# Sums of a visit taken out of PSUM by ScalarE and added by GpSimd, and the shift and scale accumulated in PSUM

## The chip, the cores and the metric

The kernel runs on one core of a Trainium2 chip. The metric is the device time of one execution in microseconds (us). Three executions of the kernel before took 1558.4, 1559.89 and 1560.08 us; the median is 1559.89 us. Engines are named as in the profile: PE is TensorE, PEld its weight load, DVE is VectorE, ACT is ScalarE, POOL is GpSimd, SP is SyncE, whose queue issues the transfers.

## The reference, cut to what matters

One decoder layer on 256 rows of 4096 numbers, all in float32:

```
mod = silu(c) @ w_ada + b_ada                       # 4096 x 12288, one row
shift, scale, gate = split(mod, 3)
h = rmsnorm(x, norm_gain) * (1 + scale) + shift     # 256 x 4096
proj = h @ w_in                                     # 4096 x 12288: q k v g_attn u_pool g_pool
y_attn = longnet_mixture(q, k, v) * silu(g_attn)    # 16 heads, 3 dilation patterns
y_pool = multiscale_pool(u_pool, w_pool, pool_scale) * silu(g_pool)
x = x + gate * (concat(y_attn, y_pool) @ w_out)     # 4096 x 4096
out = rmsnorm(x, final_gain)
```

`h` needs the first two thirds of `silu(c) @ w_ada`, and nothing of `h @ w_in` can start on a slice of `h` before shift and scale of that slice are known.

## The kernel before, in words

The 4096 columns of `h` are cut into 16 **units** of 256. For each unit the kernel needs 256 columns of shift and 256 of scale. They come from `w_ada` in 16 tasks (`ada_tasks`): a task loads two transfers of 256 KB into a `raw` tile, and later (`ada_acc`, L161) VectorE does two multiply-adds of 128x512, `aacc = raw * cact + aacc`. The 128 partial sums of each column lie on the 128 partitions. `build_h` (L203) then adds them over the partitions: four products with a column of ones on TensorE (L208, recorded as eight instructions), three small VectorE operations (L211 to L213) that make shift and scale, two ScalarE activations that make the slice of `h` in float32 (L221), and its split into a high part `hh` (ScalarE, L223) and a low part `hl` (VectorE, L224).

`h @ w_in` has 24 output chunks of 512 columns. A **piece** is 256 rows of one chunk of weights, 512 KB: one transfer into a `raw` tile, a cast to the high part `wh` (ScalarE, L237), the low part `wl = raw - wh` (VectorE, L238), and 12 products of 128x512 on TensorE (L248): eight with `wh`, then four with `wl`. There are three `wh`, three `wl` and seven `raw` buffers; the `raw` ring is shared with the tasks of `w_ada`.

The 24 chunks are **visited** in turn, round after round. A visit (L276) takes the pieces of all units that are ready and that this chunk has not had yet, and sums them in a PSUM tile `mm` of 128x1024 (two buffers). The first visit of a chunk ends with a ScalarE copy of the sums into SBUF (L289); each later one ends with a VectorE add to the sums kept there (L291: `accs = mm + accs`). This phase, "phase one" below, has 327 pieces. A last round of 24 visits, in which attention and pooling are interleaved, and the output product follow.

How fast the tasks of `w_ada` are asked for is set by a table: `ada_hook` is called once per piece, adds `2 * RATES[units built]` to a credit, and issues tasks while the credit is positive; a task costs `0.728 * 2 = 1.456`. When the last task of a unit has been issued, `build_h` is called, and two pieces later the unit is ready (`LAG`). With the table of before, `build_h` is called for units 1, 2, 3, 4, ... 15 after 14, 29, 52, 77, ... 325 pieces, and that is also where the products L208 stand among TensorE's instructions.

The order on each engine is made by a scheduler with its own cost model when the program is built. An engine then works through its own instructions strictly in that order, and an instruction that has to wait holds up all that stand behind it on its engine.

```
RATES = (0.8, 0.8, 0.8, 0.5, 0.46, 0.5, 0.5, 0.5, 0.48, 0.5, 0.5, 0.54)
ADA_COST = 0.728 * PIECE
```

Of the kernel before, what the change touches and what calls it, by code (L numbers as in the profile page):

```python
# [7 lines left out]
F32 = mybir.dt.float32  # L8
F32R = mybir.dt.float32r
AF = mybir.ActivationFunctionType  # L10
ALU = mybir.AluOpType
AX = mybir.AxisListType

P = 128
S = 256
NT = S // P
D = 4096
KT = D // P
CH = 512
# [8 lines left out]
NU = len(UNITS)  # L28
US = [sum(UNITS[:i]) for i in range(NU + 1)]
HB = 2  # L30
A0 = 1
WIN = 5
LAG = 2
RATES = (0.8, 0.8, 0.8, 0.5, 0.46, 0.5, 0.5, 0.5, 0.48, 0.5, 0.5, 0.54)
DEPTH = 3
HOLD = 1
EARLY = 4
# [18 lines left out]
def tile_hybrid_block(  # L56
# [17 lines left out]
    nc = tc.nc  # L74
    PSUM = bass.MemoryType.PSUM

    const = ctx.enter_context(tc.tile_pool(name="const", bufs=1))
# [12 lines left out]
    def misc():  # L90
        return ps_m.tile([P, CH], F32, name="psm")

    def raw_tile():
        return strm.tile([P, RAW], F32, name="raw", bufs=RAWB)
# [7 lines left out]
    ident = const.tile([P, P], F32, name="ident")  # L102
# [1 line left out]
    colB = const.tile([P, 2 * KT], F32, name="colB")  # L104
    ones_r = const.tile([P, P], F32R, name="ones_r")
    cact = const.tile([P, KT], F32, name="cact")
    ones = const.tile([P, 1], F32, name="ones")
    gb = const.tile([P, KT], F32, name="gb")
    ssq = const.tile([P, NT, 8], F32, name="ssq")
    rr = const.tile([P, NT], F32, name="rr")  # L110
# [5 lines left out]
    adap = ada_cm.enter_context(tc.tile_pool(name="ada", bufs=2, side="right"))  # L116
# [6 lines left out]
    NR = 3 * KT + 16  # L123
    nc.sync.dma_start(out=rows[0:KT], in_=c.rearrange("b (k p) -> (b k) p", p=P))
    nc.sync.dma_start(out=ident, in_=k_ident)
    nc.vector.memset(ones, 1.0)
    pt = misc()
    nc.tensor.transpose(out=pt[:, 0:KT], in_=rows[0:KT], identity=ident[0:KT, 0:KT])
    nc.scalar.activation(out=cact, in_=pt[:, 0:KT], func=AF.Silu)
# [25 lines left out]
    def ada_acc(acc, rt, kts, width, init=None):  # L155
        for i, kt in enumerate(kts):
            r = rt[:, i * width:(i + 1) * width]
            if kt == 0 and init is None:
                nc.vector.tensor_scalar(out=acc, in0=r, scalar1=cact[:, 0:1], scalar2=None, op0=ALU.mult)
            else:  # L160
                nc.vector.scalar_tensor_tensor(out=acc, in0=r, scalar=cact[:, kt:kt + 1],  # L161
                                               in1=init if kt == 0 else acc,
                                               op0=ALU.mult, op1=ALU.add)
# [3 lines left out]
    def late_work(f, lag=None):  # L167
        delayed.append(f)
        while len(delayed) > (HOLD if lag is None else lag):
            delayed.pop(0)()  # L170

    def flush_work():
        while delayed:
            delayed.pop(0)()

    def ada_tasks(u, pool):
        w = 2 * UNITS[u] * P
        n = RAW // w
        cs = slice(US[u] * P, US[u + 1] * P)
        acc = []  # L180
        tasks = []
        for a in range(0, KT, n):
            kts = list(range(a, min(KT, a + n)))

            def f(kts=kts):
                if not acc:
                    acc.append(pool.tile([P, 2 * HB * P], F32, name="aacc")[:, 0:w])
                rt = raw_tile()
                m = len(kts)
                v = rt[:, 0:m * w].rearrange("p (n s d) -> p n s d", n=m, s=2)  # L190
                if m == 1:
                    nc.sync.dma_start(out=v[:, 0], in_=wa_v[:, kts[0], 0:2, cs])
                else:
                    for i in range(2):
                        nc.sync.dma_start(out=v[:, :, i], in_=wa_v[:, kts[0]:kts[-1] + 1, i, cs])
                late_work(lambda: ada_acc(acc[0], rt, kts, w))
            tasks.append(f)
        return acc, tasks
# [4 lines left out]
    def build_h(u, acc, pool, xT):  # L203
        flush_work()
        uk, k0 = UNITS[u], US[u]
        pc = misc()
        for j in range(2 * uk):
            nc.tensor.matmul(pc[:, j:j + 1], lhsT=acc[:, j * P:(j + 1) * P], rhs=ones, start=True, stop=True)  # L208
        s12 = const.tile([P, 2, HB], F32, name="s12", bufs=2)
        ks = slice(k0, k0 + uk)  # L210
        nc.vector.tensor_tensor(out=s12[:, 0, 0:uk], in0=pc[:, 0:uk], in1=colB[:, ks], op=ALU.add)  # L211
        nc.vector.tensor_tensor(out=s12[:, 1, 0:uk], in0=pc[:, uk:2 * uk], in1=gainc[:, ks], op=ALU.mult)
        nc.vector.tensor_tensor(out=s12[:, 1, 0:uk], in0=s12[:, 1, 0:uk], in1=gb[:, ks], op=ALU.add)  # L213
        for a in range(0, uk, 2):
            kk = k0 + a
            if kk % HB == 0:
                htile[kk // HB] = [pool.tile([P, HB, S], F32R, name=n, align_bytes=LINE) for n in ("hh", "hl")]
            hh, hl = [v[:, kk % HB:kk % HB + 2] for v in htile[kk // HB]]
            hf = strm.tile([P, 2, S], F32, name="hf")
            for i in range(2):  # L220
                nc.scalar.activation(out=hf[:, i], in_=xT[:, kk + i], func=AF.Identity,  # L221
                                     scale=s12[:, 1, a + i:a + i + 1], bias=s12[:, 0, a + i:a + i + 1])
            nc.scalar.copy(out=hh, in_=hf)  # L223
            nc.vector.tensor_tensor(out=hl, in0=hf, in1=hh.bitcast(F32), op=ALU.subtract)  # L224
            for i in range(2):
                hs[kk + i] = (hh[:, i], hl[:, i])

    def split_piece(src, n, spare=False):
        rt = raw_tile()
        v = rt.rearrange("p (k n) -> p k n", n=CH)  # L230
        nc.sync.dma_start(out=v[:, 0:n], in_=src)
        if spare:
            wh, wl = [slot_a([P, PIECE, CH], F32R) for _ in range(2)]
        else:
            wh = strm.tile([P, PIECE, CH], F32R, name="wh", bufs=WHB, align_bytes=LINE)
            wl = strm.tile([P, PIECE, CH], F32R, name="wl", bufs=WLB, align_bytes=LINE)
        nc.scalar.copy(out=wh[:, 0:n], in_=v[:, 0:n])  # L237
        nc.vector.tensor_tensor(out=wl[:, 0:n], in0=v[:, 0:n], in1=wh[:, 0:n].bitcast(F32), op=ALU.subtract)  # L238
        return wh, wl

    def products(pt, hv, wh, wl, first, last):
        n = len(hv)
        seq = [(t, i, p, wh) for i in range(n) for t in range(NT) for p in range(2)]
        seq += [(t, i, 0, wl) for t in range(NT) for i in range(n)]
        for e, (t, i, p, w) in enumerate(seq):
            started = first and not any(q[0] == t for q in seq[:e])
            ended = last and not any(q[0] == t for q in seq[e + 1:])
            nc.tensor.matmul(pt[t], lhsT=hv[i][p][:, t * P:(t + 1) * P], rhs=w[:, i], start=started, stop=ended)  # L248
# [5 lines left out]
    def tick(n):  # L254
        for f in hooks:
            f(n)
        for ch in list(chains):
            ch.pop(0)()
            if not ch:
                chains.remove(ch)  # L260
        if pending and len(chains) < DEPTH and not (chains and pending[0][0] == "alone"):
            ch = pending.pop(0)
            if ch[0] == "alone":
                ch.pop(0)
            ch.pop(0)()
            if ch:
                chains.append(ch)
# [6 lines left out]
    accs = {}  # L274

    def visit(ch, ka, kb):  # L276
        pt = ps.tile([P, NT, CH], F32, name="mm")
        npc = -(-(kb - ka) // PIECE)
        szs = [(kb - ka) // npc + (1 if i < (kb - ka) % npc else 0) for i in range(npc)]
        k = ka  # L280
        for n in szs:
            wh, wl = split_piece(wi_v[:, k:k + n, ch * CH:(ch + 1) * CH], n)
            hv = [hs[k + i] for i in range(n)]
            products([pt[:, t] for t in range(NT)], hv, wh, wl, k == ka, k + n == kb)
            k += n
            tick(n)
        if ka == 0:
            accs[ch] = (slot_b if 8 <= ch < 16 else slot_a)([P, NT, CH])
            nc.scalar.copy(out=accs[ch], in_=pt)  # L289
        else:  # L290
            nc.vector.tensor_tensor(out=accs[ch], in0=pt, in1=accs[ch], op=ALU.add)  # L291

# [51 lines left out]
    for u in range(A0):  # L344
        build_h(u, first[u][0][0], hp, xT)
# [3 lines left out]
    state = {"ready": A0, "built": A0, "cur": ada_tasks(A0, adap), "credit": 0.0, "age": 0}  # L349

    def ada_hook(n):
        st = state
        st["credit"] += n * RATES[min(st["built"], len(RATES) - 1)]
        st["age"] += 1
# [17 lines left out]
    while state["ready"] < NU:  # L372
        c = ptr % NCH
        ptr += 1
        ka, kb = done[c], US[state["ready"]]
        if ka < kb:
            done[c] = kb
            visit(order[c], ka, kb)
            used[c] = kb
        else:  # L380
            ada_hook(1.0)
# [359 lines left out]
```

## Time and profile before

| | |
|---|---|
| median of three executions | 1559.89 us |
| the profiled execution | 1562.59 us |
| its span, first to last instruction | 1560.8 us |
| PE busy | 1513.5 us (97%) |
| PEld busy | 1259.0 us (81%) |
| DVE busy | 1409.9 us (90%) |
| ACT busy | 703.6 us (45%) |
| POOL busy | 0.7 us |
| granted TensorE clock, mean | 0.996 |
| DMA, mean | 315 GB/s |

Busy time on PE is the union of its instructions' records. A product of 128x512 has a record of 391 ns, yet the next one begins 227 ns after it: two are in flight at a time. So an idle PE of a few tenths of a microsecond is not seen in the busy time, and lost time in phase one is better read by counting products between two marks of the chain of waits.

### The profile page before, as it was taken

The numbers are of one execution on the slowest core, as the hardware profiler recorded it, in microseconds if no ns is written. First come the engines' busy times: TensorE is split into PE (matmuls) and PEld (weight loads), VectorE is DVE, ScalarE is ACT, GpSimd is POOL, SyncE is SP. The second block draws the span as 40 slices with busy tenths as digits, with TensorE's granted clock in tenths as the row PEclk, the third lists the DMA queues.
The fourth block names the chain that finished last, engine by engine and source line by source line (L and its number), as shares of the span: only waits on it lengthen the run. The fifth ranks groups of instructions, "written<-read, shape, count | busy, mean of one in ns | idle before, by whom it ended". The sixth has DMA issues, their size and how long they took to land.

```text
span 1560.8 us, 20366 instructions
## 1 busy us (share of the span) xinstructions
PE 1513.5 (97%) x7043; PEld 1259.0 (81%) x7043; DVE 1409.9 (90%) x1766; ACT 703.6 (45%) x830; POOL 0.7 (0%) x5
## 2 busy tenths in 40 slices
PE   2999999999999999999999999999999999999997
PEld 2877888888888888888888888888898888888875
DVE  5888999999999999899999998999988889988886
ACT  5655343443443434344344344566654444444444
POOL 0000000000000000000000000000000000000000
PEclk9999999999999999999999999999999999999999
DMA  9999999999999999999999998977678999998886
GB/s 330 348 337 356 320 330 324 321 314 338 319 318 328 309 330 310 309 314 328 350 342 324 332 330 305 319 259 231 212 247 269 308 329 358 348 321 325 324 313 258
DMA packets 324087, 491.11 MB, mean 315 GB/s; under 512 B 19320, under 2 KB 150664, under 8 KB 323984
## 3 DMA queue, kind: packets, MB, share of 16 engines
q1 hardware_dynamic: 323984, 489.82, 92.6%
q8 instruction: 55, 0.90, 0.2%
q14 instruction: 48, 0.39, 0.1%
HBM read 485.55 MB, written 4.19 MB: 314 GB/s over the span
## 4 chain that ended last, share of the span: by engine, by line
PE 88%; DVE 4%; DMA 4%; issue 2%; ACT 1%; SPq 1%; DVEq 0%; ACTq 0%
PE mm L248 80%; DMA raw<-in_w_ada_dram 3%; DVE aacc L161 2%; DVE wl L238 1%; PE psm L618 1%; PE psm L248 1%; PE psm L208 1%; PE psm L524 0%; PE psm L523 0%; PE psm L522 0%; DMA raw<-in_w_in_dram 0%; DMA sb<-in_x_dram 0%; PE psm L435 0%; DMA raw<-in_w_out_dram 0%; ACT wh L237 0%
## 5 line engine op out<-in xcount | busy, mean ns | idle before, releaser
L237 ACT CAST wh<-raw 128x1024 fp32r<-128x1024 f32 x514 | 538.4, 1050 | 688.4 <-PE mm L248 547.4
L238 DVE TENSOR_TENSOR wl<-raw,wh 128x1024 fp32r<-128x1024 f32 x514 | 624.5, 1218 | 33.6 <-ACT wh L237 31.6
L248 PE MATMUL mm<-wh,hh 128*128 128x512 f32 x1536 | 604.4, 393 | 5.4 <-ACT wh L237 4.3
L248 PE MATMUL mm<-wh,hl 128*128 128x512 f32 x1536 | 600.1, 391 | 0.0
L248 PE MATMUL mm<-wl,hh 128*128 128x512 f32 x1536 | 414.2, 391 | 0.7 <-DVE wl L238 0.6
L161 DVE SCALAR_TENSOR_TENSOR aacc<-raw,cact,aacc 128x512 f32<-128x512 f32 x496 | 370.9, 748 | 30.2 <-DMA raw<-in_w_ada_dram 22.7
L248 PEld LDWEIGHTS mm<-wh,hh 128*128 128x128 f32 x1536 | 288.8, 188 | 66.8 <-ACT wh L237 7.3
L248 PEld LDWEIGHTS mm<-wl,hh 128*128 128x128 f32 x1536 | 288.4, 188 | 61.3 <-DVE wl L238 1.6
L248 PEld LDWEIGHTS mm<-wh,hl 128*128 128x128 f32 x1536 | 288.9, 188 | 58.2
L248 PE MATMUL mm<-wh,sa 128*128 128x512 f32 x896 | 221.7, 389 | 0.0
L161 DVE SCALAR_TENSOR_TENSOR gacc<-raw,cact,gacc 128x512 f32<-128x512 f32 x248 | 185.6, 748 | 24.9 <-DMA raw<-in_w_ada_dram 21.2
L248 PEld LDWEIGHTS mm<-wh,sa 128*128 128x128 f32 x896 | 168.0, 188 | 34.9
L248 PE MATMUL mm<-wl,sa 128*128 128x512 f32 x448 | 119.8, 389 | 0.0
L291 DVE TENSOR_TENSOR sa<-mm,sa 128x1024 f32<-128x1024 f32 x92 | 112.1, 1218 | 8.6 <-PE mm L248 8.4
L248 PEld LDWEIGHTS mm<-wl,sa 128*128 128x128 f32 x448 | 84.0, 188 | 17.6 <-DVE wl L238 0.2
L291 DVE TENSOR_TENSOR sb<-mm,sb 128x1024 f32<-128x1024 f32 x48 | 58.5, 1219 | 7.3 <-PE mm L248 7.3
L328 PE MATMUL psm<-diag_r,sb 128*128 128x128 f32 x128 | 17.8, 310 | 15.6 <-DVE diag_r L320 15.6
L328 PEld LDWEIGHTS psm<-diag_r,sb 128*128 128x128 f32 x128 | 17.5, 225 | 15.8 <-DVE diag_r L320 15.8
L221 ACT ACTIVATE hf<-xT,s 128x256 f32<-128x256 f32 x32 | 17.5, 594 | 26.0 <-DVE s L213 26.0
L289 ACT COPY sa<-mm 128x1024 f32<-128x1024 f32 x16 | 16.3, 1016 | 15.1 <-PE mm L248 15.1
L672 ACT ACTIVATE yo<-sb 128x512 f32<-128x512 f32 x16 | 10.0, 626 | 25.0 <-DVE sb L670 25.0
L248 PE MATMUL psm<-wh,sa 128*128 128x512 f32 x80 | 20.1, 393 | 0.6 <-ACT wh L237 0.6
(118 smaller groups left out, 632.7 us busy)
## 6 DMA issues: line engine op xcount, KB each, us to landing
raw<-in_w_in_dram SPq DMA_DIRECT2D x384, 512.0 KB, 5.6
raw<-in_w_ada_dram SPq DMA_DIRECT2D x512, 256.0 KB, 5.4
raw<-in_w_ada_dram SPq DMA_DIRECT2D x128, 512.0 KB, 6.0
raw<-in_w_out_dram SPq DMA_DIRECT2D x128, 512.0 KB, 6.4
sb<-in_x_dram SPq DMA_DIRECT2D x16, 512.0 KB, 6.0
raw<-in_w_pool_dram SPq DMA_DIRECT2D x8, 512.0 KB, 4.4
out_dram<-sb SPq DMA_DIRECT2D x16, 256.0 KB, 2.6
fg<-in_final_gain_dram SPq DMA_DIRECT2D x8, 256.0 KB, 4.7
```

The costliest lines, as they stand in the source:

```text
L161: nc.vector.scalar_tensor_tensor(out=acc, in0=r, scalar=cact[:, kt:kt + 1], in1=init if kt == 0 else acc, op0=ALU.mult, op1=ALU.add)
L208: nc.tensor.matmul(pc[:, j:j + 1], lhsT=acc[:, j * P:(j + 1) * P], rhs=ones, start=True, stop=True)
L221: nc.scalar.activation(out=hf[:, i], in_=xT[:, kk + i], func=AF.Identity, scale=s12[:, 1, a + i:a + i + 1], bias=s12[:, 0, a + i:a + i + 1])
L237: nc.scalar.copy(out=wh[:, 0:n], in_=v[:, 0:n])
L238: nc.vector.tensor_tensor(out=wl[:, 0:n], in0=v[:, 0:n], in1=wh[:, 0:n].bitcast(F32), op=ALU.subtract)
L248: nc.tensor.matmul(pt[t], lhsT=hv[i][p][:, t * P:(t + 1) * P], rhs=w[:, i], start=started, stop=ended)
L289: nc.scalar.copy(out=accs[ch], in_=pt)
L291: nc.vector.tensor_tensor(out=accs[ch], in0=pt, in1=accs[ch], op=ALU.add)
L328: nc.tensor.matmul(px[:, i * S + t * P:i * S + (t + 1) * P], lhsT=xs[q][:, t, (2 * a + i) * P:(2 * a + i + 1) * P], rhs=diag_r[:, t], star ...
L618: nc.tensor.matmul(pt[t], lhsT=h[:, t * P:(t + 1) * P], rhs=w, start=False, stop=last and e == len(seq) - 1)
L672: nc.scalar.activation(out=y[:, t], in_=xc[:, t], func=AF.Square, accum_out=ss2[:, t, n:n + 1])
```

## The change

Three edits go together.

1. The partial sums of shift and scale of units 1 to 15 are accumulated in a PSUM tile (`misc()`, name `psm`) and no longer in SBUF. `build_h` copies them to SBUF with ScalarE (`aflat`), TensorE transposes them in four blocks of 128x128, and VectorE adds over the free axis (`tensor_reduce`). Unit 0 is still accumulated in SBUF, and takes the same four transposes and the same reduction. The column of ones goes.
2. The sums of a visit that is neither a chunk's first one nor in the last round leave PSUM by two ScalarE copies of 128x512 (`part`, two buffers), and GpSimd adds each half to the sums in SBUF. 118 of 143 visits of phase one are of this kind; before, phase one had 140 visits, and 116 of them ended with the VectorE add. The last round keeps the VectorE add.
3. The rate is 0.62 in the first five entries of the table.

```diff
-RATES = (0.8, 0.8, 0.8, 0.5, 0.46, 0.5, 0.5, 0.5, 0.48, 0.5, 0.5, 0.54)
+RATES = (0.62, 0.62, 0.62, 0.62, 0.62, 0.5, 0.5, 0.5, 0.48, 0.5, 0.5, 0.54)
...
-                    acc.append(pool.tile([P, 2 * HB * P], F32, name="aacc")[:, 0:w])
+                    acc.append((adap.tile([P, 2 * HB * P], F32, name="aflat") if u < A0 else misc())[:, 0:w])
...
-        pc = misc()
+        if u >= A0:
+            flat = adap.tile([P, 2 * HB * P], F32, name="aflat")
+            nc.scalar.copy(out=flat[:, 0:2 * uk * P], in_=acc)
+            acc = flat
+        pt = misc()
         for j in range(2 * uk):
-            nc.tensor.matmul(pc[:, j:j + 1], lhsT=acc[:, j * P:(j + 1) * P], rhs=ones, start=True, stop=True)
+            nc.tensor.transpose(out=pt[:, j * P:(j + 1) * P], in_=acc[:, j * P:(j + 1) * P], identity=ident)
+        pc = const.tile([P, 2 * HB], F32, name="pc", bufs=2)
+        nc.vector.tensor_reduce(out=pc[:, 0:2 * uk], in_=pt[:, 0:2 * uk * P].rearrange("p (j d) -> p j d", d=P),
+                                axis=AX.X, op=ALU.add)
...
+        elif state["ready"] < NU:
+            for t in range(NT):
+                part = adap.tile([P, CH], F32, name="part")
+                nc.scalar.copy(out=part, in_=pt[:, t])
+                nc.gpsimd.tensor_tensor(out=accs[ch][:, t], in0=part, in1=accs[ch][:, t], op=ALU.add)
         else:
             nc.vector.tensor_tensor(out=accs[ch], in0=pt, in1=accs[ch], op=ALU.add)
```

What the scheduler makes of it is shown at unit 5, which is built after piece 100 before and after piece 98 now. On TensorE before, the products with the ones stand between two visits (`mm_2708` and `mm_2774` are the PSUM tiles of the visits):

```order
L248 MATMUL mm_2708<-wh_2734,hl_2236 128x512
L248 MATMUL mm_2708<-wl_2735,hh_2235 128x512 x4
L208 MATMUL psm_2757<-ones_75,aacc_2262 128x1 x4
L248 MATMUL mm_2774<-wh_2777,hh_1668 128x512
L248 MATMUL mm_2774<-wh_2777,hl_1669 128x512
```

In the changed program four transposes stand there, between the first and the second piece of one visit (`mm_2919`):

```order
L253 MATMUL mm_2919<-wh_2922,hl_1868 128x512
L253 MATMUL mm_2919<-wl_2923,hh_1867 128x512 x4
L210 MATMUL psm_2947<-ident_70,aflat_2945 128x128 x4
L253 MATMUL mm_2919<-wh_2967,hh_2355 128x512
L253 MATMUL mm_2919<-wh_2967,hl_2356 128x512
```

They stand one for one where the products stood, but they wait for the ScalarE copy `aflat_2945` and no longer for VectorE itself. On ScalarE before, nothing but casts lies between one unit's slices of `h` and the next one's:

```order
L237 CAST wh<-raw 128x1024 x26
L221 ACTIVATE hf<-xT,s_2231 128x256 x2
L223 CAST hh<-hf 128x512
L237 CAST wh<-raw 128x1024 x22
L221 ACTIVATE hf<-xT,s_2762 128x256 x2
```

On ScalarE now, at the same unit, the copies of the sums stand among the casts, and the copy `aflat` behind the two copies of the visit that ended last (`mm_2871`):

```order
L242 CAST wh_2922<-raw_2920 128x1024
L242 CAST wh_2967<-raw_2965 128x1024
L298 COPY part_2913<-mm_2871 128x512
L298 COPY part_2916<-mm_2871 128x512
L206 COPY aflat_2945<-psm_2405 128x512
L242 CAST wh_2996<-raw_2994 128x1024
L242 CAST wh_3014<-raw_3012 128x1024
```

So the cast of a later piece, `wh_2996`, now stands behind copies that wait for the end of a visit. On VectorE before, the adds of the visits (L291) stand between the low parts `wl` and the multiply-adds, here at unit 5:

```order
L238 TENSOR_TENSOR wl<-raw,wh 128x1024
L161 SCALAR_TENSOR_TENSOR aacc<-raw,cact,aacc 128x512 x2
L211 TENSOR_TENSOR s_2762<-psm,colB 128x2
L212 TENSOR_TENSOR s_2762<-psm,colA 128x2
L291 TENSOR_TENSOR sa<-mm,sa 128x1024
L213 TENSOR_TENSOR s_2762<-s_2762,gb 128x2
L238 TENSOR_TENSOR wl<-raw,wh 128x1024
L161 SCALAR_TENSOR_TENSOR aacc<-raw,cact,aacc 128x512 x2
```

On VectorE now, at the same unit, the adds are gone, the multiply-adds go to PSUM, and a reduction waits for the transposes:

```order
L243 TENSOR_TENSOR wl<-raw,wh 128x1024
L157 TENSOR_SCALAR psm<-raw,cact 128x512
L212 TENSOR_REDUCE pc<-psm 128x4
L243 TENSOR_TENSOR wl<-raw,wh 128x1024
L216 TENSOR_TENSOR s_2954<-pc,colB 128x2
L217 TENSOR_TENSOR s_2954<-pc,colA 128x2
L159 SCALAR_TENSOR_TENSOR psm<-raw,cact,psm 128x512
L218 TENSOR_TENSOR s_2954<-s_2954,gb 128x2
```

GpSimd, which before had one memset in the whole program, now has 236 adds, two for each visit.

## Rows read from the trace of the kernel before

**Rows 1.** The page, part 1: busy time of each engine.

```profile
PE 1513.5 (97%) x7043; PEld 1259.0 (81%) x7043; DVE 1409.9 (90%) x1766; ACT 703.6 (45%) x830; POOL 0.7 (0%) x5
```

**Rows 2.** Stretches: length, busy time by engine, granted clock, DMA share, GB/s.

```profile
20.00:40.00 20.00, 11.48 (x90) 11.49 (x91) 15.75 (x26) 11.25 (x24) 0.00 (x0) 1.00 1.09 361
...
49.00:137.00 88.00, 84.21 (x366) 67.52 (x364) 76.64 (x92) 53.03 (x55) 0.00 (x0) 0.98 1.03 346
137.00:202.00 65.00, 63.65 (x282) 52.09 (x282) 61.94 (x71) 29.12 (x30) 0.00 (x0) 1.00 0.98 332
...
271.00:594.00 323.00, 323.00 (x1448) 268.25 (x1447) 307.04 (x348) 130.80 (x132) 0.00 (x0) 1.00 0.97 322
```

**Rows 3.** The chain of waits in order of time: start, length, what.

```profile
49.18 29.98 PE mm L248 x132
...
101.41 1.22 DVE wl L238
102.63 0.67 DVE aacc L161
...
116.02 7.62 DMA raw<-in_w_in_dram
...
136.43 0.80 PE psm L208 x8
...
201.89 0.79 PE psm L208 x8
202.68 68.13 PE mm L248 x300
...
659.31 3.78 DMA raw<-in_w_ada_dram
...
956.77 0.79 PE psm L208 x8
...
1097.10 0.87 PE psm L411 x8
```

**Rows 4.** Groups of VectorE from 49 to 957 us: count, busy, mean ns, idle before.

```profile
L238 DVE TENSOR_TENSOR wl<-raw,wh 128x1024 fp32r<-128x1024 f32 x326 | 396.3, 1218 | 16.6 <-ACT wh L237 15.9
L161 DVE SCALAR_TENSOR_TENSOR aacc<-raw,cact,aacc 128x512 f32<-128x512 f32 x462 | 345.4, 748 | 21.6 <-DMA raw<-in_w_ada_dram 15.1
L291 DVE TENSOR_TENSOR sa<-mm,sa 128x1024 f32<-128x1024 f32 x75 | 91.4, 1218 | 6.7 <-PE mm L248 6.7
L291 DVE TENSOR_TENSOR sb<-mm,sb 128x1024 f32<-128x1024 f32 x40 | 48.7, 1218 | 5.9 <-PE mm L248 5.9
```

**Rows 5.** The SP queue's waits over the whole span: total us, times, longest.

```profile
SPq L231 <- DVE wl L238: 327.3, 277, 4.8
```

**Rows 6.** ScalarE's waits from 60 to 202 us, the longest.

```profile
ACT wh L237 <- DMA raw<-in_w_in_dram: 35.6, 22, 3.7
```

**Rows 7.** Groups of the whole span, shapes apart: prices of single operations.

```profile
L237 ACT CAST wh<-raw 128x1024 fp32r<-128x1024 f32 x514 | 538.4, 1050 | 688.4 <-PE mm L248 547.4 <-DMA raw<-in_w_out_dram 59.8 <-DMA raw<-in_w_in_dram 59.4
...
L224 DVE TENSOR_TENSOR hl<-hf,hh 128x512 fp32r<-128x512 f32 x16 | 10.9, 684 | 0.0
...
L332 ACT COPY xT<-psm 128x512 f32<-128x512 f32 x16 | 9.4, 585 | 9.8 <-PE psm L328 9.8
L437 DVE SCALAR_TENSOR_TENSOR sm<-attc,psm 128x384 f32<-128x384 f32 x16 | 8.7, 542 | 0.6 <-PE psm L435 0.6
...
L445 DVE SCALAR_TENSOR_TENSOR sm<-sm,attc 128x256 f32<-128x256 f32 x16 | 6.7, 417 | 0.0
L442 DVE TENSOR_REDUCE st<-sm 128x1 f32<-128x256 f32 x16 | 6.5, 408 | 0.0
...
L445 DVE SCALAR_TENSOR_TENSOR sm<-sm,attc 128x128 f32<-128x128 f32 x16 | 4.6, 286 | 0.0
L442 DVE TENSOR_REDUCE st<-sm 128x1 f32<-128x128 f32 x16 | 4.4, 277 | 0.0
...
L542 POOL MEMSET bz<- 128x512 f32 x1 | 0.5, 527 | 959.8 <-ACT hf L221 959.8
```

More of the change, by code (lines that the diff above doesn't have):

```diff
@@ L106, in tile_hybrid_block @@
     cact = const.tile([P, KT], F32, name="cact")
-    ones = const.tile([P, 1], F32, name="ones")
     gb = const.tile([P, KT], F32, name="gb")
@@ L125, in tile_hybrid_block @@
     nc.sync.dma_start(out=ident, in_=k_ident)
-    nc.vector.memset(ones, 1.0)
     pt = misc()
```

## The prediction

> **What bounds the kernel now.** The first view is the page's busy time [rows 1]: PE 97%, DVE 90%. DVE is so full that taking work off it looks worth much; the question is whether PE ever waits for it. So the second view is the stretches [rows 2]: from 271 to 594 us PE is busy all the time at granted clock 1.00, the upper of its two levels (2.4 GHz), and DVE 307 of 323 us. DVE is nearly full there and still late for nothing. Only the two stretches before 202 us show PE idle.
>
> Busy time hides small gaps, so the third view, the chain of waits [rows 3], is used as a ruler. Undisturbed, 300 products of 128x512 take 68.13 us, 0.2271 us each, so a piece (12 products) takes 2.725 us. The first product is at 49.18 us. The partition sums of units 2, 3 and 15 stand behind 29, 52 and 325 pieces. With 0.79 us for each earlier unit's sums, they should begin at 129.0, 192.5 and 945.9 us; they begin at 136.43, 201.89 and 956.77. So phase one loses 7.4 us by piece 29, 9.4 by piece 52, and 10.8 in all, with the last 1.4 behind a transfer that lands about 663 us. More than 10.8 us cannot come back in phase one from faster helpers.
>
> Why the first 52 pieces lose: at rate 0.8 a piece brings 2 x 0.8 / 1.456 = 1.10 tasks of 512 KB, so a piece asks for 2.10 x 0.524 MB in 2.725 us, 404 GB/s. The chip moved 346 there with the DMA share at 1.03 [rows 2]; the best stretch is 361. By piece 29, 61 tiles (32.0 MB) are wanted in 79 us, and 346 GB/s bring 27.3; the ring of seven tiles holds 3.7 MB, and 1.0 MB is missing, 3 us. The same shows as 35.6 us in which casts wait for weights [rows 6], and as a transfer of 7.62 us in the chain [rows 3]. DVE has its share: between 101 and 116 us the chain steps from `wl` to multiply-add and back [rows 3], and with 1.218 + 1.10 x 2 x 0.748 = 2.86 us per piece [rows 4] it is over PE's 2.725. And the two are tied: the SP queue spends 327 us waiting for `wl`, which frees the `raw` tiles [rows 5].
>
> **The change, part by part.**
>
> *Transposes for sums.* TensorE's eight instructions of 0.79 us become four transposes. The chain has eight such transposes (L411) in 0.87 us [rows 3], so four take 0.43 us. Fifteen units lie where PE is the bound: 15 x 0.36 = 5.4 us gained. Unit 0 lies in start-up with other PE work behind it: 0.
>
> *Latency of a unit.* The `aflat` copy is 0.585 us (L332, same shape from PSUM) and the reduction 0.67 us (277 and 408 ns for 128 and 256 elements, so 131 ns more per 128) [rows 7]. Shift and scale come about 1 us later, two handovers included. The lag of two pieces, 5.4 us, covers that: 0. If the cover is gone, because the copy sits behind copies that wait for a visit's end, TensorE stands still at the transposes with all products behind them; I bound that at 1.2 us, the two part copies (2 x 0.585), for 15 units: 18 us. The order speaks against most of it: at unit 5 the copies belong to the visit before, one whole piece earlier.
>
> *Accumulating in PSUM.* No row shows VectorE writing PSUM. Reading it costs nothing extra: 542 ns for 384 elements (L437), against 417 plus 131 for 256 from SBUF (L445) [rows 7]. I take 748 ns as now. A copy out of or into the other memory may differ by some 60 ns either way; 480 multiply-adds would make that 29 us of VectorE's time, spread over 900 us, of which 140 are freed. Neither end moves PE.
>
> *Adds off VectorE.* 115 adds of 1.218 us stand in phase one [rows 4]: 140 us of VectorE's time go. By the second view PE waits for none of them after 202 us, so by itself this is worth nothing there; earlier it belongs to the 9.4 us.
>
> *Copies on ScalarE.* 118 visits x 2 x 0.585 = 138 us on an engine that is 45% busy. A one-piece visit has a cast of 1.05 and two copies, 2.2 of 2.725 us: it fits. What queues behind a copy is the cast two or three pieces ahead, which has over 2.7 us to spare.
>
> *Adds on GpSimd.* The trace has no GpSimd add. The nearest row is its memset of 128x512, 527 ns, one stream [rows 7]; that is the lower end, and three streams one after the other, 1.58 us, the upper (an estimate). VectorE takes 684 ns for the shape. I take two reads in turn, 1.05 us. Two adds are 2.1 us per visit. Visits have one piece (12 of the 118), two (40), three (60) or four (6). At 1.05 all fit; at 1.58 the twelve overrun by 0.44 us each, 5 us in all. By the Trainium skill (GPSIMD Engine Reference, section 3.1) an add of 2048 elements takes 4497 ns; a quarter is an estimate of 1.12 us, beside my 1.05.
>
> *The rate.* At 0.62 a piece brings 0.85 tasks: 356 GB/s instead of 404, and VectorE needs 2.49 us per piece. By piece 98 (five units) 178 tiles, 93.3 MB, are wanted in 267 us, and 346 GB/s bring 92.4: the gap fits the ring. So both reasons for the early loss go. But unit 1 is ready after 20 pieces and not 16, so the second round opens with twelve one-piece visits and their adds where before it had two-piece ones. I count 6 of the 9.4 us as gained, since 356 is still above 346, and take nothing for the 1.4 at 663 us, where the rates are the old ones.
>
> **Sum.** New waits, of the kinds bounded above, I set at 3 us, mostly in those twelve visits. 5.4 + 6 - 3 = 8.4 us less. The profiled execution took 1562.59 (span 1560.8 and 1.8 around it), so 1554.2; it is 2.7 above the median of the runs shown, so 1551.5 us.
>
> **Rivals.**
>
> *A: the early loss stays.* If the transfers are the bound whatever VectorE does, piece 1 to 52 lose as now (the DMA share of 1.03 speaks for it; the 361 in the x loads against it), and 3 to 6 us of new waits eat the transposes. 5.4 - 3 to 5.4 - 6: about no change, 1557 to 1561.
>
> *B, slower: GpSimd's adds and VectorE's `wl` exclude each other.* Both take two inputs from SBUF. If one stands still while the other runs, a one-piece visit needs two adds and a `wl` in turn: 2 x 1.05 + 1.22 = 3.3 us against 2.725, with 1.58 even 4.4. Twelve visits: 7 to 20 us. Until piece 98 there are 22 two-piece visits; VectorE's 2 x 2.49 = 4.98 us plus one wait of half to a whole add comes to 5.5 to 6.0 against 5.45: up to 12 us. Later, at rate 0.5, 4.5 plus such a wait fits. So it costs 7 to 32 us against gains of 11.4: with the likelier ends 1570, slower by 10. It decides once a wait per visit is over 0.5 us. For it: VectorE is at 95% in the steady stretch [rows 2], so it has little to give. Against it: 140 us are freed there, and the multiply-adds, now with one operand in PSUM, may run beside an add, with 1.3 us of them per piece to hide it. No row can show it, since GpSimd does nothing before.
>
> A rule of the Trainium skill says the same (SBUF — State Buffer, section "SBUF: two separate sides"): VectorE and GpSimd share a pair of ports, held for a whole instruction, and a VectorE operation with two SBUF inputs is among those that block an add. No run here shows it. By it rival B would hold for `wl` and for nothing that reads PSUM.
>
> *C: all comes back.* The whole 10.8 and the 5.4, with no new wait: 16 us, 1543.7.
>
> *D: the transposes wait* for `aflat` at every unit, up to 18 us against 11.4: 1566. It shares B's side and is counted with it.
>
> **From the cases to the numbers.** Forecast 0.48, its own range 1546.5 to 1556.5; A 0.19; B and D 0.21; C 0.12. What a measurement of this kernel can tell from no change is about 0.2%, 3.1 us. Faster by more: the forecast, C and a little of A less the forecast's weak end, 0.61; within it 0.18; slower 0.21. The range that leaves two in ten out goes from 1544 (C) to 1567 (the near part of B).
>
> **What would show it.** In the profile after: L210 in the chain at 0.43 us each with no wait in front; PE counted by the ruler loses 3 to 5 us up to piece 56, not 9.4; casts wait less than 35.6 us for weights between 60 and 202 us; VectorE falls from 95% to some 80% between 271 and 594 us; GpSimd adds near 1.05 us. It is wrong if `wl` or an add is much longer than its price or waits beside the other, if casts wait for `part` buffers between about 125 and 160 us, or if TensorE waits for `aflat`.

## The result: 1.0% slower, and the profile after

The changed kernel takes 1575.93 us (median of four, 1571.71 to 1579.41) against 1559.99 for the kernel before; the ratio is 1.0100, 95% interval 1.0085 to 1.0114. The prediction was 1551.5 us, faster, with a range from 1544 to 1567. The profiled execution took 1579.41 us, the slowest of the four, so its span is some 3.5 us longer than that of a median run.

First the busy time by engine of the changed kernel, which answers to [rows 1]:

```profile
PE 1517.2 (96%) x6979; PEld 1249.9 (79%) x6979; DVE 1398.8 (89%) x1666; ACT 820.3 (52%) x1081; POOL 373.8 (24%) x241
```

GpSimd has taken over the adds, and yet VectorE is hardly less busy: 1398.8 us, not the 1270 that 140 us less would leave. The groups of VectorE from 49 to 975 us of the changed kernel say why; they answer to [rows 4] (the last columns are busy us, mean ns, and idle time before):

```profile
L243 DVE TENSOR_TENSOR wl<-raw,wh 128x1024 fp32r<-128x1024 f32 x329 | 488.0, 1490 | 57.2 <-ACT wh L242 55.8
L159 DVE SCALAR_TENSOR_TENSOR psm<-raw,cact,psm 128x512 f32<-128x512 f32 x463 | 347.8, 751 | 15.4 <-DMA raw<-in_w_ada_dram 8.7
L229 DVE TENSOR_TENSOR hl<-hf,hh 128x512 fp32r<-128x512 f32 x15 | 16.0, 1068 | 1.4 <-ACT hh L228 1.4
L157 DVE TENSOR_SCALAR psm<-raw,cact 128x512 f32<-128x512 f32 x14 | 10.4, 744 | 0.0
L212 DVE TENSOR_REDUCE pc<-psm 128x4 f32<-128x512 f32 x15 | 10.3, 687 | 5.0 <-PE psm L210 4.9
```

`wl` takes 1490 ns on average where it took 1218, and `hl`, 684 before, takes 1068. Both read two tensors from SBUF. The multiply-adds, with one operand in PSUM, stayed at 751. The other side of it is GpSimd's own group, and the shortest, median and longest of the same instructions:

```profile
L299 POOL TENSOR_TENSOR sa<-part,sa 128x512 f32<-128x512 f32 x156 | 243.3, 1580 | 435.6 <-ACT part L298 435.6
L299 POOL TENSOR_TENSOR sb<-part,sb 128x512 f32<-128x512 f32 x80 | 129.9, 1646 | 159.1 <-ACT part L298 159.1
```

```profile
L299 POOL TENSOR_TENSOR sa<-part,sa x156: 1261/1296/2381, 129.6 to 966.5; 128x512 f32<-128x512 f32 x156
L243 DVE TENSOR_TENSOR wl<-raw,wh x514: 1204/1221/2333, 44.2 to 1545.3; 128x1024 fp32r<-128x1024 f32 x172
L159 DVE SCALAR_TENSOR_TENSOR psm<-raw,cact,psm x465: 739/752/757, 46.5 to 955.6; 128x512 f32<-128x512 f32 x155
```

An add alone takes 1.29 us; the longest, 2.38, is an add and most of a `wl`. A `wl` alone takes 1.22; the longest, 2.33, is a `wl` and most of an add. The timeline of the one-piece visits (start, length, engine; rows of TensorE, its weight load and the queue are left out, at the dots others too) shows the alternation:

```profile
134.60 2.12 DVE L243 TENSOR_TENSOR wl<-raw,wh 128x1024 fp32r<-128x1024 f32 x1
135.59 7.01 POOL L299 TENSOR_TENSOR sb<-part,sb 128x512 f32<-128x512 f32 x4
135.68 0.59 ACT L298 COPY part<-mm 128x512 f32<-128x512 f32 x1 [0.49 <-POOL sa L299]
136.16 1.05 ACT L242 CAST wh<-raw 128x1024 fp32r<-128x1024 f32 x1
136.65 1.53 DVE L159 SCALAR_TENSOR_TENSOR psm<-raw,cact,psm 128x512 f32<-128x512 f32 x2
138.06 0.59 ACT L298 COPY part<-mm 128x512 f32<-128x512 f32 x1 [0.85 <-PE mm L253]
138.09 2.12 DVE L243 TENSOR_TENSOR wl<-raw,wh 128x1024 fp32r<-128x1024 f32 x1
...
141.57 2.12 DVE L243 TENSOR_TENSOR wl<-raw,wh 128x1024 fp32r<-128x1024 f32 x1
```

One `wl` begins every 3.48 us, and a piece of TensorE takes 2.73: here the chain of helpers is the bound. VectorE goes from `wl` to two multiply-adds and back without a pause, GpSimd runs its four adds without a gap, and a ScalarE copy waits for it (0.49 us, for a `part` buffer).

The ruler of the prediction (2.725 us a piece, 0.43 for a group of transposes, first product at 48.00 us) shows where TensorE loses. The groups of transposes of units 1 to 5 and 15 stand behind 18.2, 37.2, 56.2, 74.2, 98 and 323 pieces:

```profile
98.38 0.60 PE L210 MATMUL psm<-ident,aflat 128*128 128x128 f32 x4
156.27 0.66 PE L210 MATMUL psm<-ident,aflat 128*128 128x128 f32 x4 [0.18 <-ACT aflat L206]
217.29 0.60 PE L210 MATMUL psm<-ident,aflat 128*128 128x128 f32 x4
275.02 0.66 PE L210 MATMUL psm<-ident,aflat 128*128 128x128 f32 x4 [0.17 <-ACT aflat L206]
342.24 0.60 PE L210 MATMUL psm<-ident,aflat 128*128 128x128 f32 x4
960.20 0.60 PE L210 MATMUL psm<-ident,aflat 128*128 128x128 f32 x4
```

Undisturbed they would begin at 97.6, 149.8, 202.0, 251.5, 316.8 and 934.2 us. So the loss up to each is 0.8, 6.5, 15.3, 23.5, 25.5 and 26.0 us, where the kernel before loses 7.4 by piece 29 and 10.8 in all. The first round of visits, without adds, is now nearly perfect; nearly everything is lost from piece 28, where the adds begin, to piece 98, where the rate falls to 0.5; after that almost nothing. The stretches of the changed kernel say the same (columns as in [rows 2]), the granted clock included, which is below 1.00 (its upper level, 2.4 GHz) in two of the stretches in which TensorE has gaps:

```profile
49.00:98.00 49.00, 49.00 (x217) 40.51 (x217) 41.80 (x47) 34.36 (x37) 0.00 (x0) 1.00 1.01 339
98.00:157.00 59.00, 55.63 (x241) 43.38 (x240) 52.78 (x57) 36.96 (x48) 26.94 (x17) 1.00 0.95 319
157.00:217.00 60.00, 55.38 (x226) 43.53 (x225) 54.87 (x57) 31.25 (x45) 33.42 (x22) 0.94 0.91 299
217.00:275.00 58.00, 54.12 (x223) 41.59 (x222) 54.59 (x56) 29.00 (x42) 26.85 (x19) 0.97 0.93 309
275.00:342.00 67.00, 66.25 (x288) 53.20 (x289) 61.16 (x62) 36.23 (x49) 25.59 (x20) 1.00 0.95 318
342.00:960.00 618.00, 617.24 (x2742) 510.71 (x2741) 568.80 (x597) 333.26 (x425) 257.29 (x159) 1.00 0.98 329
```

From 157 to 275 us the DMA share falls to 0.91 and 0.93: the transfers are no longer the bound, they wait for `raw` tiles that VectorE frees late.

The largest single losses stand behind the builds of units 2 and 3. At unit 3, whose transposes are at 217.29 us, the last small operation of the build (L218, two tensors from SBUF) is held up by an add; ScalarE waits for it before it makes the slice of `h`, and the cast that TensorE needs next stands behind that slice (rows between these are left out):

```profile
220.97 3.28 POOL L299 TENSOR_TENSOR sa<-part,sa 128x512 f32<-128x512 f32 x2 [3.40 <-ACT part L298]
221.77 1.27 DVE L218 TENSOR_TENSOR s<-s,gb 128x2 f32<-128x2 f32 x1
223.08 1.09 ACT L226 ACTIVATE hf<-xT,s 128x256 f32<-128x256 f32 x2 [1.69 <-DVE s L218]
224.08 1.03 ACT L242 CAST wh<-raw 128x1024 fp32r<-128x1024 f32 x1
225.16 0.50 PE L253 MATMUL mm<-wh,hh 128*128 128x512 f32 x1 [2.06 <-ACT wh L242]
```

L218 takes 1.27 us there, where its median is 0.155. TensorE stands still for 2.06 us, and for 2.03 us at the same place behind unit 2's build, just before 165.62 us. Right behind both stops the granted clock is low:

```profile
165.00:170.00 5.00, 4.38 (x10) 3.48 (x11) 4.36 (x5) 3.95 (x6) 3.01 (x2) 0.50 0.76 234
225.00:230.00 5.00, 4.84 (x14) 3.84 (x15) 4.83 (x5) 3.48 (x6) 3.01 (x2) 0.66 0.79 251
```

A share of 0.50 is the lower of the two levels (1.2 GHz). In these two places 19 products begin some 0.43 us apart instead of 0.227, which is 3.8 us. The two stops and the slower products are about 8 of the 26 us.

The rest of the program is longer as well. After the last group of sums the kernel before runs 604.2 us, with the last 59 pieces (the end of phase one and the last round) to come; the changed one 617.4 with 61. Less the group (0.79 and 0.43) and two pieces (5.45), that is 603.4 against 611.5.

### The profile page after: what moved, and what is told of

It is laid out like the page before. It is cut to its first block, busy times and chain, and to the rows that moved or that the text cites. A ratio compares the mean times of both kernels' runs of the same rounds, so it can differ in the third digit from the quotient of the medians.

```text
span 1577.6 us, 20712 instructions
## 1 busy us (share of the span) xinstructions
PE 1517.2 (96%) x6979; PEld 1249.9 (79%) x6979; DVE 1398.8 (89%) x1666; ACT 820.3 (52%) x1081; POOL 373.8 (24%) x241
## 4 chain that ended last, share of the span: by engine, by line
PE 74%; DVE 9%; DMA 9%; issue 4%; ACT 2%; POOL 0%; SPq 0%; DVEq 0%; ACTq 0%
PE mm L253 69%; DMA raw<-in_w_ada_dram 8%; DVE wl L243 4%; DVE psm L159 1%; DVE gacc L159 1%; PE psm L628 1%; ACT wh L242 1%; DMA raw<-in_w_in_dram 1%; PE psm L253 1%; DMA raw<-in_w_out_dram 1%; PE psm L421 0%; PE psm L462 0%; POOL sb L299 0%; PE psm L210 0%; PE psm L445 0%
## 5 line engine op out<-in xcount | busy, mean ns | idle before, releaser
L243 DVE TENSOR_TENSOR wl<-raw,wh 128x1024 fp32r<-128x1024 f32 x514 | 713.1, 1393 | 70.6 <-ACT wh L242 67.7
L159 DVE SCALAR_TENSOR_TENSOR psm<-raw,cact,psm 128x512 f32<-128x512 f32 x465 | 349.3, 751 | 15.6 <-DMA raw<-in_w_ada_dram 8.7
L299 POOL TENSOR_TENSOR sa<-part,sa 128x512 f32<-128x512 f32 x156 | 243.3, 1580 | 435.6 <-ACT part L298 435.6
L298 ACT COPY part<-mm 128x512 f32<-128x512 f32 x236 | 127.9, 589 | 110.6 <-PE mm L253 106.3
L299 POOL TENSOR_TENSOR sb<-part,sb 128x512 f32<-128x512 f32 x80 | 129.9, 1646 | 159.1 <-ACT part L298 159.1
L159 DVE SCALAR_TENSOR_TENSOR aflat<-raw,cact,aflat 128x512 f32<-128x512 f32 x31 | 23.3, 752 | 8.8 <-DMA raw<-in_w_ada_dram 7.9
```

Of the source, the lines that this page charges most:

```text
L298: nc.scalar.copy(out=part, in_=pt[:, t])
L299: nc.gpsimd.tensor_tensor(out=accs[ch][:, t], in0=part, in1=accs[ch][:, t], op=ALU.add)
```

## The experiments

Theory 1 is rival B of the prediction: GpSimd's adds and VectorE's operations with two inputs from SBUF exclude each other. Theory 2 holds the rate of 0.62 responsible on whatever engine the adds run. Theory 3 is about the 8 us after phase one. "Loss" below is TensorE's loss in phase one by the ruler, worked out as above from each profile's first product and last group of sums.

**Adds back on VectorE, rate 0.62 kept.**

```diff
-        elif state["ready"] < NU:
-            for t in range(NT):
...
-                nc.gpsimd.tensor_tensor(out=accs[ch][:, t], in0=part, in1=accs[ch][:, t], op=ALU.add)
         else:
             nc.vector.tensor_tensor(out=accs[ch], in0=pt, in1=accs[ch], op=ALU.add)
```

> The changed kernel with the adds of the visits back on VectorE; transposes, accumulation in PSUM and the rate 0.62 stay. Theory 1 (GpSimd's adds and VectorE's operations with two SBUF inputs exclude each other, and that is the whole early loss): the low part wl goes back from a mean of 1.49 us to 1.22, the loss in phase one falls under the 11 us of before, and the transposes' 5 us show: 1550 to 1557 us. Theory 2 (the rate 0.62 and the later readiness of unit 1 are to blame): the loss stays, over 1568. Theory 3 (the lost 8 us after phase one come from the changed order of the last round, which the rate shifts): phase one recovers but the time stays near 1562.

Measured 1582.9 us, ratio 1.0139 (1.0124 to 1.0154), loss 34 us. All expectations but Theory 2's are off: `wl` is back at 1220 ns and the kernel is still slower, by 6 us more (by the ratios). At this rate GpSimd's adds help.

```profile
L243 DVE TENSOR_TENSOR wl<-raw,wh 128x1024 fp32r<-128x1024 f32 x327 | 397.6, 1220 | 34.3 <-ACT wh L242 32.6
L296 DVE TENSOR_TENSOR sa<-mm,sa 128x1024 f32<-128x1024 f32 x78 | 95.1, 1219 | 8.8 <-PE mm L253 8.5
```

So collisions alone are not the cause: 118 adds cost VectorE more as its own work than as collisions.

**The old rates, everything else as changed.**

```diff
-RATES = (0.62, 0.62, 0.62, 0.62, 0.62, 0.5, ...)
+RATES = (0.8, 0.8, 0.8, 0.5, 0.46, 0.5, ...)
```

> The changed kernel with the table of rates of before. Theory 1: the adds still hold up wl, and with 1.10 tasks per piece VectorE has less to spare, while the twelve one-piece visits with adds are gone; wl keeps a mean near 1.45 us, and the time is 1566 to 1590. Theory 2 (rate to blame): back to 1552 to 1560. Theory 3 (last round's order follows the rate): the part after phase one falls from 611 to about 604 us, whatever phase one does.

Measured 1555.04 us, ratio 0.9963 (0.9949 to 0.9977), loss 6 us: faster than the kernel before, 21 us faster than the changed one. Theory 1's range, 1566 to 1590, is missed. But its mechanism is there undiminished:

```profile
L243 DVE TENSOR_TENSOR wl<-raw,wh 128x1024 fp32r<-128x1024 f32 x336 | 496.4, 1482 | 41.4 <-ACT wh L242 39.6
```

`wl` is as long as in the changed kernel, and TensorE does not notice: at 0.5 VectorE has the time. Of Theory 3, the part after phase one is 606.7 us here, between the two.

**GpSimd busy as long, but reading nothing.**

```diff
-                nc.gpsimd.tensor_tensor(out=accs[ch][:, t], in0=part, in1=accs[ch][:, t], op=ALU.add)
+                for _ in range(3):
+                    nc.gpsimd.memset(part, 0.0)
```

> The changed kernel in which GpSimd does not add: for each half it writes zeros over the copied sums three times, 3 x 0.53 = 1.59 us, as long as the adds took on average, and reads nothing from SBUF. It leaves out the adds, so the sums in SBUF are those of the first visits. Theory 1, as two inputs from SBUF against an operation that reads SBUF: wl stays at 1.22 us and the time is 1550 to 1560. If any work on GpSimd blocks wl: mean wl about 1.5 us and 1570 to 1580 as with the adds. If ScalarE's copies or the two part buffers are to blame: wl at 1.22 us but still over 1566.

Measured 1556.36 us, ratio 0.9969 (0.9957 to 0.9980), loss 4.5 us. Theory 1's first case, as expected: the rate of 0.62 does no harm once neither a GpSimd operation that reads SBUF nor an add of its own takes VectorE's time.

```profile
L243 DVE TENSOR_TENSOR wl<-raw,wh 128x1024 fp32r<-128x1024 f32 x336 | 409.4, 1223 | 127.3 <-ACT wh L242 119.6 <-PE mm L253 2.6 <-DMA raw<-in_w_ada_dram 1.5
L300 POOL MEMSET part<- 128x512 f32 x708 | 338.9, 526 | 608.0 <-ACT part L298 606.8
```

ScalarE's copies and the two `part` buffers are therefore not the cause; they are the same here.

**The adds alone, in the kernel before.** The diff is the second edit of the change and nothing else.

> The kernel before with the adds of the visits through ScalarE and GpSimd alone: shift and scale stay in SBUF and the rates are the old ones. Theory 1: the multiply-adds, now again with two tensors from SBUF, are held up by adds as wl is (mean over 0.85 us instead of 0.75), nothing is left beside which an add can run, and the time is 1590 to 1650. If only wl is held up: multiply-adds at 0.75 us and 1570 to 1590, as with old rates in the changed kernel.

Measured 1632.59 us, ratio 1.0458 (1.0442 to 1.0473), loss 77 us. This is Theory 1 at its clearest: with the sums of shift and scale in SBUF again, the multiply-adds read two tensors from SBUF, and they are held up too.

```profile
L238 DVE TENSOR_TENSOR wl<-raw,wh 128x1024 fp32r<-128x1024 f32 x325 | 489.7, 1518 | 13.5 <-ACT wh L237 13.0
L161 DVE SCALAR_TENSOR_TENSOR aacc<-raw,cact,aacc 128x512 f32<-128x512 f32 x462 | 467.0, 1011 | 10.6 <-DMA raw<-in_w_ada_dram 3.4
```

1011 ns against 751 with the sums in PSUM. So the first edit is what makes the second bearable.

**Rate 0.62 alone, in the kernel before.** The diff is the line of the table.

> The kernel before with rate 0.62 in the first five entries alone. With the adds on VectorE a one-piece visit asks it for 1.22 + 1.27 + 1.22 = 3.7 us in 2.73, and a two-piece visit for 6.2 in 5.45 until piece 98: 12 x 1.0 + 22 x 0.75 = 28 us. Theory 2 (the rate is the culprit on any engine): 1575 to 1592. If the rate hurts only together with GpSimd's adds: within 5 us of before.

Measured 1574.1 us, ratio 1.0085 (1.0070 to 1.0100), loss 21 us. Theory 2 is right in sign: the rate costs 13 us even without GpSimd. The 28 us that were worked out stand against the loss of 21, not against the 13: the rate also removes early loss (none is left by the first group of sums, where the kernel before has lost 4 us). Why 21 and not 28 is not shown; the slack of three `wl` buffers was left out of the 28.

**The first edit alone, old rates, adds on VectorE.** The diff is the first edit of the change.

> The kernel before with the first edit alone: accumulation in PSUM, transposes and reduction; adds of the visits on VectorE, old rates. If the transposes are worth 0.36 us at each of 15 units and nothing else changes: 5 us less than before, about 1556 to 1557, and then GpSimd's adds are worth 1 to 2 us at the old rates (1555.0 with them). If VectorE's longer build of a unit (a reduction of 0.69 us more, and 0.27 us more for the first product of a unit into PSUM) matters where VectorE is nearly full: 1560 to 1566, and the adds on GpSimd are what brings the gain at the old rates.

Measured 1556.73 us, ratio 0.9977 (0.9964 to 0.9989): 4.0 us gained, where the transposes were to bring 5.4; loss 12 us, much as before. GpSimd's adds are worth some 2 us on top of it at the old rates, which the two intervals do not separate (0.9964 to 0.9989 here, 0.9949 to 0.9977 there).

The next two take the changed kernel and separate what 0.62 brings with it: the one-piece visits of the second round, and the higher rate of units 3 and 4.

**No adds in one-piece visits** (24 of 236 left out).

```diff
+                if kb - ka > 2:
-                nc.gpsimd.tensor_tensor(out=accs[ch][:, t], in0=part, in1=accs[ch][:, t], op=ALU.add)
+                    nc.gpsimd.tensor_tensor(out=accs[ch][:, t], in0=part, in1=accs[ch][:, t], op=ALU.add)
```

> The changed kernel at rate 0.62, in which the twelve one-piece visits of the second round copy their sums out but add nothing: 24 of 236 GpSimd adds are left out, and so a term of the output's sums. Old rates brought 21 us back, and a GpSimd that reads nothing 20, so rate and collisions act together. Theory 4 (the one-piece visits make the loss: two adds of 1.3 us and a wl of 1.22 in turn every 2.73 us): most of the 20 us come back, 1556 to 1561. Theory 5 (the higher rate of units 3 and 4 does: two-piece visits with 2 x 2.49 us of VectorE work plus a wait of 0.9 in 5.45): only 7 to 9 us of it, 1566 to 1570.

Measured 1562.67 us, ratio 1.0010 (1.0000 to 1.0020), loss 15 us: 13 of the 20 us come back with a tenth of the adds, 7 stay. Neither theory alone; both parts, two to one. The stop behind unit 2's build shrinks to 0.42 us, the one behind unit 3's stays at 2.05 us, with the fall of the clock behind it.

**Rates 0.8, 0.8, 0.8, 0.62, 0.62.** No one-piece visit has an add, units 3 and 4 are asked for at 0.62.

```diff
-RATES = (0.62, 0.62, 0.62, 0.62, 0.62, 0.5, ...)
+RATES = (0.8, 0.8, 0.8, 0.62, 0.62, 0.5, ...)
```

> The changed kernel with rates 0.8, 0.8, 0.8, 0.62, 0.62 and the rest as it is: the second round opens with two-piece visits again, no one-piece visit has an add, but units 3 and 4 are asked for at 0.62; phase one shrinks to 110 visits with 86 GpSimd adds of sums. Theory 4 (one-piece visits): no slower than with the old rates, 1550 to 1557. Theory 5 (higher rate of units 3 and 4): VectorE falls behind between 130 and 300 us, 1562 to 1575.

Measured 1560.49 us, ratio 0.9999 (0.9987 to 1.0011), loss 14 us. Between the two ranges, like the run before: 15 us better than the changed kernel, 5 worse than with the old rates, although it has 86 adds of sums and not 118.

**Rates 0.75, 0.75, 0.75, 0.5, 0.46**, a version meant to beat both kernels.

```diff
-RATES = (0.62, 0.62, 0.62, 0.62, 0.62, 0.5, ...)
+RATES = (0.75, 0.75, 0.75, 0.5, 0.46, 0.5, ...)
```

> The changed kernel with rates 0.75, 0.75, 0.75, 0.5, 0.46 and the rest as it is, meant to keep what 0.62 gains before 137 us (fewer bytes asked for) without what it loses after: two one-piece visits with adds instead of twelve, and the slow rates of before for units 3 and 4. If the loss at 0.62 comes from one-piece visits and from the higher rate of units 3 and 4: 1552 to 1556, at or a little under the old rates (1555.0). If any lowering of the first rates costs, since it raises the number of visits (148 against 140): 1557 to 1563.

Measured 1555.35 us, ratio 0.9967 (0.9956 to 0.9977), loss 6 us. It is as fast as the old rates and not faster; both beat the kernel before by 0.3 to 0.4%, and they are the best versions found that compute everything.

**Memsets at the old rates.** The diff is that of the memsets, with the old table.

> The changed kernel with the rates of before, and three memsets of the copied half in place of each GpSimd add (the adds are left out). It shows what the collisions still cost at the old rates. If the stretched wl (mean 1.48 us) is covered there, as TensorE's unbroken run after 200 us says: 1552 to 1555, no more than 3 us under old rates. If the collisions cost there as at 0.62: 1535 to 1548.

Measured 1555.92 us, ratio 0.9968 (0.9957 to 0.9980), loss 5 to 6 us. Without any collision the time is that with them (1555.04), a little above the range given. At the old rates collisions cost nothing that these runs can tell; at 0.62 they cost 20 us.

**A copy in place of the add, rate 0.62.**

```diff
-                nc.gpsimd.tensor_tensor(out=accs[ch][:, t], in0=part, in1=accs[ch][:, t], op=ALU.add)
+                nc.gpsimd.tensor_copy(accs[ch][:, t], part)
```

> The changed kernel at rate 0.62 in which GpSimd copies each half into the place of the sums and does not add it: one input from SBUF in place of two; the adds are left out. It asks what in a GpSimd operation blocks VectorE. If any read from SBUF does: wl still shows lengths of 1.22 plus the rest of a copy (mean 1.30 to 1.45 us), and the time lies between 1556 and 1576 by the copy's length (0.5 to 0.8 us against 1.29). If only two inputs do: mean wl 1.22 us, 1555 to 1558, as with the memsets.

Measured 1552.27 us, ratio 0.9948 (0.9935 to 0.9961), loss 2.5 us. Outside both expectations: the mean of `wl` stays at 1229 ns, as if only two inputs blocked, but the copies are held up.

```profile
L243 DVE TENSOR_TENSOR wl<-raw,wh 128x1024 fp32r<-128x1024 f32 x338 | 413.9, 1229 | 116.7 <-ACT wh L242 113.5
L299 POOL COPY sa<-part 128x512 f32<-128x512 f32 x156 | 121.8, 807 | 547.4 <-ACT part L298 547.4
```

```profile
L299 POOL COPY sa<-part x156: 605/616/1681, 129.6 to 942.9; 128x512 f32<-128x512 f32 x156
L243 DVE TENSOR_TENSOR wl<-raw,wh x514: 1204/1221/1668, 44.3 to 1517.8; 128x1024 fp32r<-128x1024 f32 x172
```

A copy alone takes 0.61 us and up to 1.68, the longest `wl` 1.67. So a read of one input collides too. That a copy seldom stands in the way of `wl` fits its being half as long, beside multiply-adds of 0.75 us; no run separates the two.

## Why the prediction was wrong, point by point

**What failed is one term: "New waits, of the kinds bounded above, I set at 3 us".** By the ruler the changed kernel loses 26 us in phase one; the prediction left 4.8 of the old loss and added 3. The new waits are about 25, not 3. Part of it is the 0 in "Latency of a unit": the lag of two pieces, 5.4 us, was to cover the build, but at units 2 and 3 an add held up the build's own small operations, the low part `hl` was ready 10.8 us (unit 3) and 12.2 us (unit 2) after the transposes began, and TensorE stopped for 2 us and then ran for some microseconds at the lower clock, for which the prediction has no term. Rival B named their mechanism, their place (one-piece visits and two-piece visits up to piece 98) and a price of 7 to 32 us; it had the smaller chance, and its time, 1570, is still 6 us short of the measured one.

**Why the wrong case was taken.** Two arguments stood against B, and both failed. "140 us are freed there": true, but 92 us of it went back at once into longer `wl` (488.0 us of them against 396.3, [rows 4]), so that VectorE is busy 92% from 342 to 960 us (568.80 of 618) and not the 80% forecast. "The multiply-adds may run beside an add": true as well, at 751 ns they are never held up; but the two adds of a visit come in a row, 2.6 us, and only 1.3 us of multiply-adds per piece stand between two `wl`. The second add overlaps a `wl` in 110 of 118 visits. In the timeline above the period is 3.48 us; B's formula with the measured add, 2 x 1.29 + 1.22, gives 3.8, with the guessed one 3.3. The rest is a small overlap: nearly every `wl` that began during one add ended 1.08 us after it, where it takes 1.22 alone, so two such handovers leave 3.5.

**What excludes what.** The runs show `wl` at 1.22 us alone and 2.33 at most behind an add; multiply-adds at 1011 ns on average with both tensors in SBUF, and in the changed kernel never over 757 ns with one in PSUM; beside memsets `wl` stays at 1223 ns. So VectorE's operations with two SBUF inputs and a GpSimd operation that reads SBUF take turns, for a whole instruction but for about 0.14 us. The Trainium skill's rule (SBUF — State Buffer, "SBUF: two separate sides") says this of the two engines' shared ports, and these runs agree. Two inputs are not the only case: with the adds alone in the kernel before, the first product of a unit, with one input and its output both in SBUF, went from 480 ns to 1514 at most, while the same product into PSUM stayed at 754 or less in the changed kernel.

**The rate.** Its reasoning on the transfers was right as far as it went: up to piece 18 the loss is 0.8 us, and with copies, which seldom hold up `wl`, or memsets, which never do, the kernel at 0.62 takes 1552.3 and 1556.4 us, 1 to 5 us over the forecast. The prediction is about the time of this change without collisions, in part by luck: phase one loses 2.5 and 4.5 us there, where the sum left 7.8, and the rest of the program is some 4 and 9 us longer than the 603.4 of the kernel before, which the sum did not expect. What it missed is that the rate acts on VectorE twice: 12 one-piece visits, each with a full set of adds for one piece of TensorE work, and 2.49 us of VectorE work per piece up to piece 98, where an add's wait no longer fits. Both were in the text, as rival B; they were not in the sum. A table of the four cases shows how the parts act on each other (medians in us, from sets in which the kernel before took 1560.0 to 1561.9):

| | old rates | rate 0.62 |
|---|---|---|
| kernel before | 1560.7 | 1574.1 |
| first edit | 1556.7 | 1582.9 |
| first and second edit | 1555.0 | 1575.9 |
| the same, GpSimd only writes | 1555.9 | 1556.4 |

The rate costs 13 to 26 us in the first three rows and nothing in the last. That the first edit makes the rate dearer (13 to 26) was not tested by itself; a unit's build asks VectorE for 0.69 us of reduction and 0.26 us more for the first product into PSUM, which does not add up to 13 us over five units. The traces show where a part of it lies. With the adds on VectorE and rate 0.62, `aflat` stands on ScalarE behind casts that wait themselves (2.33 us for a transfer at unit 3, 1.71 us for `wl` at unit 4), and TensorE waits for it 1.40 and 1.13 us there; it also falls to the lower clock twice (0.68 from 195 to 200 us, 0.73 from 230 to 235), while with the rate alone the clock stays at 1.00 in phase one. The rest stays open.

**The smaller terms.** Transposes: 0.43 us a group, as forecast, and no unit's `aflat` held TensorE for more than 0.2 us in the changed kernel (rival D is out there; with the adds on VectorE its wait does appear); the first edit alone gained 4.0 of the 5.4 us. Accumulating in PSUM: 751 against 748 ns, as taken, and far inside the 60 ns allowed either way. The reduction: 687 ns against 0.67 us. A GpSimd add: 1.29 us, not 1.05; within the bounds, and at the old rates without effect. ScalarE's copies: 589 ns each, with little effect.

**The last 8 us stay open.** After phase one the changed kernel takes 611.5 us in its profiled run against 603.4; both of these runs are about 3 us over their median, so that does not explain it. By the same count the first edit alone takes 602.8, the old rates 606.7, rate 0.62 alone 606.4, and memsets at 0.62, with no collision at all, 612.1. So the collisions are not needed for it. That rate and GpSimd each add a few us through the order in which the last round and the output product are laid out is a guess: the copies at 0.62 take 607.3 us there, 5 less than the memsets, and one profile of each does not settle it.

## What to carry to other kernels

Before work is moved from VectorE to GpSimd, list what VectorE will run beside it: each of its operations with two SBUF tensors will take turns with a GpSimd operation that reads SBUF, so the cost is a sum in that stretch, not a maximum, and here it decided where VectorE's slack in a visit was under one GpSimd add of 1.29 us (an estimate from the rows: 0.5 us in a two-piece visit at rate 0.62, 1.4 us in a three-piece one at 0.5). An operand moved to PSUM takes an operation out of that contest (1011 to 751 ns here). And a rate or a lookahead that was set for one division of work has to be set again with the new one: the same edits at the old rates were 0.4% faster, at the new one 1.0% slower.

## What the runs showed of the hardware

- A GpSimd add of 128x512 in float32 takes 1.29 us alone, a copy 0.61, a memset 0.53. The Trainium skill's GPSIMD Engine Reference (section 3.1) led to an estimate of 1.12 us for the add; the measurement decides.
- A held-up instruction is recorded as a longer one and not as idle time: `wl` 1.22 to 2.33 us, an add 1.26 to 2.38. Busy time on VectorE hid the loss; shortest and median beside the mean show it.
- The first product of a unit (`raw` times a scalar, 128x512) takes 480 ns into SBUF and 744 into PSUM; the multiply-add takes 748 into SBUF and 751 into PSUM.
- Behind two stops of about 2 us in the changed kernel TensorE's granted clock was low (0.50 from 165 to 170 us, 0.66 from 225 to 230), and products began 0.43 us apart instead of 0.227. Not every such stop shows it: with the adds on VectorE TensorE stood still for 1.99 us before 165.33 us, and the clock was 1.00 from 160 to 170.
